# Attention of a two-layer encoder: copies alternate bank by bank between ScalarE and VectorE, one reciprocal per group, a new order of the score matmuls, and four engines in program order

## The chip, the cores and the metric

The kernel runs on one core of a Trainium2 chip. The metric is the device time of one execution in microseconds (us). Before the change the median of three runs is 2476.0 us (2475.49 to 2480.37).

## What is computed

One step of a two-layer encoder on 1024 prompt rows and 32 sample rows of width 1024: layer 0 has a matrix-memory mixer and an MLP, layer 1 a banded attention and an MLP. The change is in the attention. Each chunk of 64 queries sees its own 64 keys and the 512 before them; 16 query heads share 4 key/value heads (4 query heads to one), of width 64:

```python
def one_chunk(args):
    ci, qb = args
    kb = lax.dynamic_slice_in_dim(kp, ci * CHUNK, span, axis=1)
    vb = lax.dynamic_slice_in_dim(vp, ci * CHUNK, span, axis=1)
    s = jnp.einsum('bqkgd,bskd->bkgqs', qb, kb).astype(jnp.float32) * (HD_B ** -0.5) + bias
    valid = (ci * CHUNK - BAND + jnp.arange(span)) >= 0
    s = jnp.where(valid, s, -jnp.inf)
    p = jax.nn.softmax(s, axis=-1).astype(vb.dtype)
    return jnp.einsum('bkgqs,bskd->bqkgd', p, vb)
```

The 32 sample rows are treated as one more chunk against 512 cached keys and their own 32.

## The kernel before

The kernel is one program: layer 0, the projections q, k and v, the attention, its output projection, and layer 1's MLP. TensorE makes the matmuls, ScalarE (ACT) and VectorE (DVE) empty PSUM and do the softmax, GpSimd (POOL) normalises, and SP issues the loads.

The attention runs over `gp` (two pairs of key heads) and, within one, over 17 chunks `c` (16 is the sample chunk). The list `wide, slim` sets the order: wide chunks (8 to 15, with 576 keys) alternate with slim ones (0 to 7 with 64 to 512 keys, and 16), so gp 0 runs 8, 7, 12, 6, 13, 5, 14, 4, 15, 16, 9, 3, 10, 2, 11, 1, 0. A chunk has two groups, `e` = 0 and 1, one for each key head. A group has two units of 128 rows (two query heads by 64 queries; the sample chunk has one unit). So there are 34 chunks, 68 groups and 132 units.

For each unit, `softmax_unit` makes: the scores `s` (TensorE, two matmuls for each part, since q and k are kept as a high and a low part; a width over 512 takes two PSUM banks), a VectorE instruction that adds the bias and takes the row's minimum of the negated, scaled sum into `mx` (L1569, called the bias instruction below), the exponential with its row sum on ScalarE (L1572), a reciprocal of that sum on VectorE (L1573), and the multiplication by it on GpSimd (L1574). The scores have two PSUM buffers, so a unit's matmuls wait until the bias instruction of the unit two before has read its buffer.

For each group, `transposed` turns the probabilities `p` in blocks of 128 keys on TensorE into `pt`, two blocks of keys to a PSUM bank, with three such buffers; a copy then brings each bank to SBUF (`pT`). All copies of a group with e = 0 are VectorE's (L1598), all with e = 1 ScalarE's (L1596). A wide group has five key tiles, so three banks (0, 1 and 2); a slim group one to three.

For each chunk, `weighted_values` multiplies `pT` of both groups with V into `pv` (one PSUM buffer), key tile by key tile with the two groups in turn; every matmul shows as two instructions. ScalarE casts the result to a high part (L1613), and VectorE subtracts that for the low part (L1614).

`Flow` sets the order: a group is added as a generator, and each tick goes on with all groups, oldest first. So in step n stand the values of the chunk whose second group is n-4, then the transposes of group n-3, then the scores of group n. Only TensorE keeps this order (`manual_schedule`); for ScalarE, VectorE and GpSimd a scheduler sets the order when the program is built. Twice in gp 1, `wo_block` loads a block of the output weights (raw_ob) and splits it into two parts (w_ob) for the projection that follows.

Of the kernel before, what the change touches and what calls it, by code (L numbers as in the profile page):

```python
# [8 lines left out]
F32 = mybir.dt.float32  # L9
F32R = mybir.dt.float32r  # L10
# [65 lines left out]
def trunk_kernel(ctx: ExitStack, tc: tile.TileContext, a, o):  # L76
# [7 lines left out]
    def raw_tile(shape, name):  # L84
        return ring.tile(shape, F32, tag="raw", name=name, bufs=3)

    def split(dst_h, dst_l, src, eng=None):

        nc.scalar.copy(dst_h, src)
        (eng or nc.vector).tensor_sub(dst_l, src, dst_h.bitcast(F32))  # L90
# [706 lines left out]
    def tmp_t(shape, name, dt=F32):  # L797
        return T_.tile(shape, dt, tag="t", name=name, bufs=5)
# [299 lines left out]
    class Rooms:  # L1098


        def __init__(self):
            self.free = []
# [309 lines left out]
    def qo(c):  # L1412
        return QOT[c // 6][:, :, :, c % 6, :]
# [135 lines left out]

    nun = [0]  # L1550

    def softmax_unit(qst, g, k0, nk, bt, off, nm):

        s = psT.tile([P, 2, 512], F32, tag="s", name=f"s_{nm}", bufs=2)
        parts = [(0, 0, nk)] if nk <= 512 else [(0, 0, nk // 2), (1, nk // 2, nk // 2)]
        for b, j0, w in parts:
            for i in range(2):
                nc.tensor.matmul(s[:, b, :w], qst, kk[i][:, g, k0 + j0:k0 + j0 + w], start=(i == 0), stop=(i == 1))  # L1558
# [9 lines left out]
        mx = at.tile([P, 4], F32, tag="mx", name=f"mx_{nm}", bufs=8)  # L1568
        nc.vector.tensor_tensor_reduce(out=z.rearrange("p (b w) -> p b w", b=np_), in0=s[:, :np_, :w],  # L1569
                                       in1=bt.rearrange("p (b w) -> p b w", b=np_), op0=ALU.add, op1=ALU.min,  # L1570
                                       scale=-0.125, scalar=3e38, accum_out=mx[:, 0:1])
        nc.scalar.activation(z, z, AF.Exp, bias=mx[:, 0:1], scale=-1.0, accum_out=mx[:, 2:3])  # L1572
        nc.vector.reciprocal(mx[:, 3:4], mx[:, 2:3])  # L1573
        nc.gpsimd.tensor_scalar(z, z, mx[:, 3:4], 1.0, op0=ALU.mult, op1=ALU.mult)  # L1574
        return p

    def transposed(ps_, wid, e, nm):

        nt = (wid + P - 1) // P
        nq = len(ps_) * P  # L1580
        pt_sb = ring.tile([P, 5, 256], F32, tag="wc", name=f"pT_{nm}_{e}", bufs=6)
        for j0 in range(0, nt, 2):
            pt = psT.tile([P, 2, 256], F32, tag="pt", name=f"pt_{nm}_{e}_{j0}", bufs=3)
            js = range(j0, min(nt, j0 + 2))
            for j in js:
                kp = min(P, wid - j * P)
                for pr in range(len(ps_)):
                    nc.tensor.transpose(pt[:kp, j - j0, pr * P:(pr + 1) * P], ps_[pr][:, j * P:j * P + kp], ident)  # L1588
            if wid >= (js[-1] + 1) * P:
                jss = [(j0, len(js), P)]  # L1590
            else:
                jss = [(j, 1, min(P, wid - j * P)) for j in js]
            for j, m, kp in jss:
                dst, src = pt_sb[:kp, j:j + m, :nq], pt[:kp, j - j0:j - j0 + m, :nq]
                if e:
                    nc.scalar.copy(dst, src)  # L1596
                else:
                    nc.vector.tensor_copy(dst, src)  # L1598
        return pt_sb

    def weighted_values(gp, pts, nq, wid, vt0, dst, nm):
        nt = (wid + P - 1) // P
        pv = psT.tile([P, 256], F32, tag="pv", name=f"pv_{nm}", bufs=1)
        for j in range(nt):
            kp = min(P, wid - j * P)
            for e in range(2):
                g = 2 * gp + e
                nc.tensor.matmul(pv[64 * e:64 * e + 64, :nq], V[:kp, vt0 + j, g * 64:(g + 1) * 64], pts[e][:kp, j, :nq],  # L1608
                                 start=(j == 0), stop=(j == nt - 1))
# [3 lines left out]
        nc.scalar.copy(hi, src)  # L1613
        nc.vector.tensor_sub(lo, src, hi.bitcast(F32))  # L1614

    def att_group(gp, c, e):

        g = 2 * gp + e
        nm = f"{gp}_{c}"
        if c < 16:  # L1620
            nk = min(c + 1, 9) * 64
            k0 = max(0, c - 8) * 64
            off = k0 % P
            wid, vt0 = off + nk, (k0 - off) // P
            pr_ = [softmax_unit(qo(c)[:, e, gp, pr * P:(pr + 1) * P], g, k0, nk, bias[2 * g + pr][:, 576 - nk:], off,
                                f"{nm}_{e}{pr}") for pr in range(2)]
        else:
            wid, vt0 = 544, 8
            pr_ = [softmax_unit(qo(16)[:, e, gp, 0:P], g, TP, 544, sbias[g], 0, f"{nm}_{e}")]
        yield  # L1630
        yield
        yield
        pts[gp, c, e] = transposed(pr_, wid, e, nm)
        yield
        if e:
            if c < 16:
                dst = lambda hl: qo(c)[:, hl, gp, :]
            else:
                dst = lambda hl: qo(16)[:, hl, gp, :].rearrange("p (r i) -> p r i", i=64)[:, :, :TS]
            weighted_values(gp, [pts[gp, c, i] for i in range(2)], len(pr_) * P, wid, vt0, dst, nm)  # L1640
    pts = {}
    wo = a["w_out_b"][0]
    wo_pre = {}

    def wo_block(pr, half):
        cols = wo[:, 256 * pr:256 * pr + 256]
        return wtile(f"ob{pr}_{half}", lambda raw: [
            (raw[64 * e:64 * e + 64], cols[(2 * half + e) * 256:(2 * half + e + 1) * 256].rearrange(
                "(r d) c -> d r c", d=64)) for e in range(2)])

    wide, slim = (8, 12, 13, 14, 15, 9, 10, 11), ((7, 6, 5, 4, 16, 3, 2, 1, 0), (16, 7, 6, 5, 4, 3, 2, 1, 0))
    with tc.manual_schedule(engines={mybir.EngineType.PE}):
        for gp in range(2):
            for i in range(17):
                c = slim[gp][i // 2] if i % 2 else wide[i // 2] if i < 16 else slim[gp][8]
                for e in range(2):
                    flow.add(att_group(gp, c, e))
                    flow.tick()  # L1660
                if gp and i in (8, 11):
                    wo_pre[0, len(wo_pre)] = wo_block(0, len(wo_pre))
        flow.finish()
    psT_cm.__exit__(None, None, None)
    at_cm.__exit__(None, None, None)
    kv_cm.__exit__(None, None, None)
# [132 lines left out]
```

## Time and profile before

| | us |
|---|---|
| median of three runs | 2476.0 |
| the profiled execution | 2479.81 |
| its span | 2478.0 |
| attention, from the first scores to the first matmul of the output projection | 1422.1 to 1632.1 |
| TensorE busy, over the span | 2413.7 |

The profile gives starts in us from the start of the span. A busy TensorE is not one at its peak, since a matmul's shown length overlaps with the next one's; how fast it goes is read from the starts. The chain of waits follows the work that ended last back from the end, and so shows at each moment which engine is waited for. PE is TensorE's matmuls, PEld its weight loads.

### The profile page before, as it was taken

To read this page: it belongs to the slowest core of one execution; us is meant where nothing else is said; L and a number is where in the kernel's file an instruction comes from. 1 tells how busy PE (TensorE), PEld (TensorE's weight loads), DVE (VectorE), ACT (ScalarE), POOL (GpSimd) and SP (SyncE) were. 2 spreads that over 40 slices of the span, in tenths; PEclk is the share of its full clock that TensorE was granted. 3 is DMA by queue.
4 is the path that set the end of the run, shared out by engine and by line. 5 is a ranking of instruction groups with operands and counts; after the bars stand their busy time and mean duration, and the time that the engine had idled before them with its cause. 6 is when DMAs were issued, how large, how long until landed. Compare 5 with 4: busy or idle time off the path is not lost.

```text
span 2478.0 us, 42688 instructions
## 1 busy us (share of the span) xinstructions
PE 2413.7 (97%) x16844; PEld 2315.4 (93%) x16844; DVE 1759.7 (71%) x4038; ACT 1016.9 (41%) x2118; POOL 168.6 (7%) x315
## 2 busy tenths in 40 slices
PE   7999999999999999999999999999999999999997
PEld 4999999999999999999999867789999999899997
DVE  4899999788679679677597667746853442776758
ACT  4644456382211212212266556654754443221212
POOL 0211100000000000000001134410000000000003
PEclk9999999999999999999999989999999999999999
DMA  8433224313224224234122310050375646767632
GB/s 297 122 110 101 84 88 129 107 35 119 77 87 137 84 86 135 80 92 142 43 98 82 91 40 1 18 147 27 134 251 212 215 179 254 262 239 273 255 130 72
DMA packets 236220, 318.10 MB, mean 128 GB/s; under 512 B 11624, under 2 KB 185084, under 8 KB 234996
## 3 DMA queue, kind: packets, MB, share of 16 engines
q1 hardware_dynamic: 236020, 315.38, 38.8%
q8 instruction: 132, 2.16, 0.4%
q14 instruction: 68, 0.56, 0.1%
HBM read 242.79 MB, written 74.91 MB: 128 GB/s over the span
## 4 chain that ended last, share of the span: by engine, by line
PE 78%; DVE 8%; DMA 6%; ACT 2%; issue 1%; POOL 0%; SPq 0%; DVEq 0%; POOLq 0%; ACTq 0%
PE up L118 10%; PE up L120 10%; PE up L119 9%; PE dn L1283 9%; PE dn L119 5%; PE dn L118 5%; PE dn L120 5%; DMA fx<-hd 3%; PE pv L1608 2%; PE pt L1588 2%; PE s L1558 2%; PE o L118 1%; PE o L119 1%; PE o L120 1%; PE op_b L118 1%
## 5 line engine op out<-in xcount | busy, mean ns | idle before, releaser
L120 PE MATMUL up<-u,w_up 128*128 128x264 f32 x1024 | 292.9, 286 | 0.0
L118 PE MATMUL up<-u,w_up 128*128 128x264 f32 x1024 | 292.4, 286 | 0.0
L119 PE MATMUL up<-u,w_up 128*128 128x264 f32 x1024 | 291.1, 284 | 0.0
L1283 PE MATMUL dn<-fx,wf 128*128 128x264 f32 x2208 | 275.3, 286 | 7.9 <-DMA fx<-hd 7.4
L1283 PEld LDWEIGHTS dn<-fx,wf 128*128 128x128 f32 x2208 | 272.2, 189 | 9.7 <-issue 4.6
L119 PE MATMUL dn<-h,w_dn 128*128 128x384 f32 (+1 forms) x768 | 249.5, 325 | 0.0
L118 PE MATMUL up<-U,w_up 128*128 128x384 f32 (+1 forms) x768 | 249.2, 324 | 0.0
L119 PE MATMUL up<-U,w_up 128*128 128x384 f32 (+1 forms) x768 | 247.9, 323 | 0.0
L118 PE MATMUL dn<-h,w_dn 128*128 128x384 f32 (+1 forms) x768 | 247.8, 323 | 0.0
L120 PE MATMUL up<-U,w_up 128*128 128x384 f32 (+1 forms) x768 | 247.6, 322 | 0.0
L120 PE MATMUL dn<-h,w_dn 128*128 128x384 f32 (+1 forms) x768 | 247.3, 322 | 0.0
L119 PEld LDWEIGHTS up<-u,w_up 128*128 128x128 f32 x1024 | 193.9, 189 | 0.0
L118 PEld LDWEIGHTS up<-u,w_up 128*128 128x128 f32 x1024 | 193.8, 189 | 0.0
L120 PEld LDWEIGHTS up<-u,w_up 128*128 128x128 f32 x1024 | 193.3, 189 | 0.0
L986 DVE SCALAR_TENSOR_TENSOR ACC<-dn,ada,ACC 128x264 f32<-128x264 f32 (+4 forms) x328 | 131.7, 426 | 86.4 <-PE dn L1283 74.6
L238 DVE SCALAR_TENSOR_TENSOR aacc<-rada,cs,aacc 128x256 f32<-128x256 f32 x448 | 190.3, 477 | 0.0
L986 DVE SCALAR_TENSOR_TENSOR acc<-dn,ada,acc 128x384 f32<-128x384 f32 (+2 forms) x256 | 119.4, 486 | 47.4 <-PE dn L120 46.3
L1025 ACT ACTIVATE r<-up 128x384 f32<-128x384 f32 (+1 forms) x96 | 44.3, 463 | 246.9 <-PE up L120 238.4
L119 PEld LDWEIGHTS dn<-h,w_dn 128*128 128x128 f32 x768 | 144.4, 188 | 0.2 <-DVE h L1028 0.2
L120 PEld LDWEIGHTS dn<-h,w_dn 128*128 128x128 f32 x768 | 144.5, 188 | 0.0
L120 PEld LDWEIGHTS up<-U,w_up 128*128 128x128 f32 x768 | 144.3, 188 | 0.0
L118 PEld LDWEIGHTS up<-U,w_up 128*128 128x128 f32 x768 | 144.2, 188 | 0.1
(354 smaller groups left out, 5957.4 us busy)
## 6 DMA issues: line engine op xcount, KB each, us to landing
hd<-HL SPq DMA_DIRECT2D x28, 1848.0 KB
raw_up<-in_w_up_dram SPq DMA_DIRECT2D x68, 512.0 KB
rada<-in_w_ada_dram SPq DMA_DIRECT2D x64, 512.0 KB
fx<-hd SPq DMA_DIRECT2D x37, 528.0 KB
raw_dn<-in_w_down_dram SPq DMA_DIRECT2D x36, 512.0 KB
ada_room<-in_w_ada_dram SPq DMA_DIRECT2D x32, 512.0 KB
fx<-hd SPq DMA_DIRECT2D x50, 264.0 KB
fx<-hd SPq DMA_DIRECT2D x16, 792.0 KB
```

The source lines that it names most:

```text
L118: nc.tensor.matmul(ps, wh, mov(0, k), start=(k == 0), stop=False)
L119: nc.tensor.matmul(ps, wh, mov(1, k), start=False, stop=False)
L120: nc.tensor.matmul(ps, wl, mov(0, k), start=False, stop=(k == nk - 1))
L238: nc.vector.scalar_tensor_tensor(acc[:, cnd], raw[:, k], sc, acc[:, cnd], op0=ALU.mult, op1=ALU.add)
L986: nc.vector.scalar_tensor_tensor(xs, ps[:, off + o:off + o + mm_], gate[:, fc, cnd:cnd + 1], xs, op0=ALU.mult, op1=ALU.add)
L1025: nc.scalar.activation(r, ps[:, :n], AF.Relu)
L1283: nc.tensor.matmul(p, ws[w][:, wl, k], t[:, s0, xl], start=first and k + n_ == 0, stop=k == kg - 1 and n_ == 2, skip_group_check=not first)
L1558: nc.tensor.matmul(s[:, b, :w], qst, kk[i][:, g, k0 + j0:k0 + j0 + w], start=(i == 0), stop=(i == 1))
L1588: nc.tensor.transpose(pt[:kp, j - j0, pr * P:(pr + 1) * P], ps_[pr][:, j * P:j * P + kp], ident)
L1608: nc.tensor.matmul(pv[64 * e:64 * e + 64, :nq], V[:kp, vt0 + j, g * 64:(g + 1) * 64], pts[e][:kp, j, :nq], start=(j == 0), stop=(j == nt - 1))
```

## The change

It does five things in the attention, and none elsewhere:

- The copies of transposed banks alternate between ScalarE and VectorE bank by bank, by a counter, whichever group they belong to.
- There is one reciprocal for a group, on two columns, in `normalize`. It is issued in the next step, behind the first unit's scores of the next group.
- The group's second unit of scores stands on TensorE between the first and the second bank of the older group's transposes.
- The values of a chunk come first in a step, ahead of the step's scores; before, they were ahead of the transposes, but the scores of the step before stood between them and the last transposes.
- ScalarE, VectorE and GpSimd keep program order too.

With it go 11 buffers of probabilities in turn where there were 12, one tile of `mx` for a group (6 buffers) where there was one for a unit (8), and loads of the output weights that are issued two rounds ahead of their split. The core of the diff:

```diff
-        i = nun[0] % 12
-        p = tmp_t([P, 640], f"p_{nm}") if i < 5 else raw_tile([P, 640], f"p_{nm}") if i < 8 else \
+        i = nun[0] % 11
+        p = tmp_t([P, 640], f"p_{nm}") if i < 5 else raw_tile([P, 640], f"p_{nm}") if i < 7 else \
...
-        nc.scalar.activation(z, z, AF.Exp, bias=mx[:, 0:1], scale=-1.0, accum_out=mx[:, 2:3])
-        nc.vector.reciprocal(mx[:, 3:4], mx[:, 2:3])
-        nc.gpsimd.tensor_scalar(z, z, mx[:, 3:4], 1.0, op0=ALU.mult, op1=ALU.mult)
-        return p
+        nc.scalar.activation(z, z, AF.Exp, bias=mx[:, 0:1], scale=-1.0, accum_out=mx[:, 1:2])
+        return p, z
+
+    def normalize(units, mx):
+
+        n = len(units)
+        nc.vector.reciprocal(mx[:, 2, :n], mx[:, 1, :n])
+        for i, (_, z) in enumerate(units):
+            nc.gpsimd.tensor_scalar(z, z, mx[:, 2, i:i + 1], 1.0, op0=ALU.mult, op1=ALU.mult)
...
-                if e:
+                ncopy[0] += 1
+                if ncopy[0] % 2:
                     nc.scalar.copy(dst, src)
                 else:
                     nc.vector.tensor_copy(dst, src)
-        return pt_sb
+            yield pt_sb
+    ncopy = [0]
...
-    with tc.manual_schedule(engines={mybir.EngineType.PE}):
...
+    with tc.manual_schedule(engines={ET.PE, ET.Activation, ET.DVE, ET.Pool}):
+        for n in range(len(todo) + 4):
+            new, old, done = n if n < len(todo) else None, groups.get(n - 3), groups.pop(n - 4, None)
+            if done and done.e:
+                done.values()
+            if new is not None:
+                groups[n] = Group(*todo[n][:3])
+                groups[n].scores(0)
+            if groups.get(n - 1):
+                normalize(groups[n - 1].units, groups[n - 1].mx)
+            turn = old.turn() if old else iter(())
+            next(turn, None)
+            if new is not None:
+                groups[n].scores(1)
+            for _ in turn:
+                pass
+            if new is not None and todo[n][3] == "load":
...
+                for dst, src in wo_srcs(wo_raw, 0, len(wo_pre)):
+                    nc.sync.dma_start(dst, src)
+            elif new is not None and todo[n][3]:
...
+                split(w[:, 0], w[:, 1], wo_raw)
```

What this does to the orders, at chunk 13 of gp 0. In a name, the first number is the chunk; in s, p and mx the digits that follow are group and unit (p_5_10 is chunk 5, group 1, unit 0), in pT the group, and in pt the group and the first key tile of the bank (0, 2 or 4 for banks 0, 1 and 2); the number at the end only tells buffers apart. On TensorE, up to the first values of chunk 13, there stood:

```order
L1588 MATMUL pt_13_1_4_15377<-ident,p_13_10_15267 128x128
L1588 MATMUL pt_13_1_4_15377<-ident,p_13_11_15279 128x128
L1558 MATMUL s_14_00_15381<-k_14100,QO_13704 128x288
L1558 MATMUL s_14_00_15381<-k_14101,QO_13704 128x288
L1558 MATMUL s_14_00_15381<-k_14100,QO_13704 128x288
L1558 MATMUL s_14_00_15381<-k_14101,QO_13704 128x288
L1558 MATMUL s_14_01_15392<-k_14100,QO_13704 128x288
L1558 MATMUL s_14_01_15392<-k_14101,QO_13704 128x288
L1558 MATMUL s_14_01_15392<-k_14100,QO_13704 128x288
L1558 MATMUL s_14_01_15392<-k_14101,QO_13704 128x288
L1608 MATMUL pv_13_15403<-pT_13_0_15329,V 64x256
L1608 MATMUL pv_13_15403<-pT_13_1_15364,V 64x256
```

Now there stands:

```order
L1559 MATMUL s_14_01_15356<-k_14100,QO_13704 128x288
L1559 MATMUL s_14_01_15356<-k_14101,QO_13704 128x288
L1559 MATMUL s_14_01_15356<-k_14100,QO_13704 128x288
L1559 MATMUL s_14_01_15356<-k_14101,QO_13704 128x288
L1594 MATMUL pt_13_1_2_15364<-ident,p_13_10_15233 128x128
L1594 MATMUL pt_13_1_2_15364<-ident,p_13_11_15252 128x128
L1594 MATMUL pt_13_1_2_15364<-ident,p_13_10_15233 128x128
L1594 MATMUL pt_13_1_2_15364<-ident,p_13_11_15252 128x128
L1594 MATMUL pt_13_1_4_15370<-ident,p_13_10_15233 128x128
L1594 MATMUL pt_13_1_4_15370<-ident,p_13_11_15252 128x128
L1616 MATMUL pv_13_15374<-pT_13_0_15314,V 64x256
L1616 MATMUL pv_13_15374<-pT_13_1_15349,V 64x256
```

The eight score matmuls of 14's first group have moved from the place right before the values of 13 to places between the transposes, and the last two banks of transposes now stand right before the values.

On ScalarE, from the cast of chunk 6's values to that of chunk 13's, there stood:

```order
L1613 CAST QO_13490<-pv_6_15318 128x256
L1596 COPY pT_13_1_15364<-pt_13_1_0_15365 128x512
L1596 COPY pT_13_1_15364<-pt_13_1_2_15371 128x512
L1572 ACTIVATE p_5_10_15349,mx_5_10_15350<-p_5_10_15349,mx_5_10_15350 128x384
L1572 ACTIVATE p_5_11_15358,mx_5_11_15359<-p_5_11_15358,mx_5_11_15359 128x384
L1596 COPY pT_13_1_15364<-pt_13_1_4_15377 128x256
L1572 ACTIVATE p_14_00_15386,mx_14_00_15387<-p_14_00_15386,mx_14_00_15387 128x576
L1572 ACTIVATE p_14_01_15397,mx_14_01_15398<-p_14_01_15397,mx_14_01_15398 128x576
L1613 CAST QO_13704<-pv_13_15403 128x256
```

Now there stands:

```order
L1621 CAST QO_13490<-pv_6_15293 128x256
L1572 ACTIVATE p_5_10_15308,mx_5_1_15304<-p_5_10_15308,mx_5_1_15304 128x384
L1603 COPY pT_13_0_15314<-pt_13_0_0_15315 128x512
L1572 ACTIVATE p_5_11_15324,mx_5_1_15304<-p_5_11_15324,mx_5_1_15304 128x384
L1603 COPY pT_13_0_15314<-pt_13_0_4_15333 128x256
L1572 ACTIVATE p_14_00_15343,mx_14_0_15337<-p_14_00_15343,mx_14_0_15337 128x576
L1572 ACTIVATE p_14_01_15361,mx_14_0_15337<-p_14_01_15361,mx_14_0_15337 128x576
L1603 COPY pT_13_1_15349<-pt_13_1_2_15364 128x512
L1621 CAST QO_13704<-pv_13_15374 128x256
```

The copies of group 1's banks 0 and 2 have gone to VectorE, those of group 0's banks 0 and 2 have come, and the copy of group 1's bank 1 has moved from the third place to the one right before the next cast, behind all four exponentials.

On VectorE, from the subtraction for chunk 6's values to the bias instruction of 14's second unit, there stood:

```order
L1614 TENSOR_TENSOR QO_13490<-pv_6_15318,QO_13490 128x256
L1598 COPY pT_13_0_15329<-pt_13_0_2_15336 128x512
L1598 COPY pT_13_0_15329<-pt_13_0_4_15342 128x256
L1569 ISA p_5_10_15349,mx_5_10_15350<-s_5_10_15346,bias_14913 128x384
L1569 ISA mx_5_10_15350 128x1
L1569 ISA p_5_11_15358,mx_5_11_15359<-s_5_11_15355,bias_14916 128x384
L1569 ISA mx_5_11_15359 128x1
L1569 ISA p_14_00_15386,mx_14_00_15387<-s_14_00_15381,bias_14913 128x576
L1569 ISA mx_14_00_15387 128x1
L1573 RECIPROCAL mx_5_10_15350<-mx_5_10_15350 128x1
L1569 ISA p_14_01_15397,mx_14_01_15398<-s_14_01_15392,bias_14913 128x576
```

Now there stands:

```order
L1622 TENSOR_TENSOR QO_13490<-pv_6_15293,QO_13490 128x256
L1569 ISA p_5_10_15308,mx_5_1_15304<-s_5_10_15305,bias_14913 128x384
L1569 ISA mx_5_1_15304 128x1
L1578 RECIPROCAL mx_5_0_15263<-mx_5_0_15263 128x2
L1569 ISA p_5_11_15324,mx_5_1_15304<-s_5_11_15321,bias_14916 128x384
L1569 ISA mx_5_1_15304 128x1
L1605 COPY pT_13_0_15314<-pt_13_0_2_15327 128x512
L1569 ISA p_14_00_15343,mx_14_0_15337<-s_14_00_15338,bias_14913 128x576
L1569 ISA mx_14_0_15337 128x1
L1578 RECIPROCAL mx_5_1_15304<-mx_5_1_15304 128x2
L1605 COPY pT_13_1_15349<-pt_13_1_0_15350 128x512
L1569 ISA p_14_01_15361,mx_14_0_15337<-s_14_01_15356,bias_14913 128x576
```

The rows with `mx` alone as their output bring the row minimum out. The bias instruction of chunk 5 has moved ahead of the copies, right behind the subtraction, and a reciprocal for both units of a group now stands ahead of a bank's copy.

More of the change, by code (lines that the diff above doesn't have):

```diff
@@ L1614, in weighted_values, with __init__ @@
         nc.vector.tensor_sub(lo, src, hi.bitcast(F32))
[L1616 to L1635, printed above, removed]
+    class Group:
+        def __init__(self, gp, c, e):
+            self.gp, self.c, self.e, self.g = gp, c, e, 2 * gp + e
+            self.nm = f"{gp}_{c}"
+            self.mx = at.tile([P, 3, 2], F32, tag="mx", name=f"mx_{self.nm}_{e}", bufs=6)
+            self.units = []
+            self.n = 2 if c < 16 else 1
@@ L1636, in att_group @@
             if c < 16:
[L1637 to L1640 removed]
+                self.nk, self.k0 = min(c + 1, 9) * 64, max(0, c - 8) * 64
+                self.off = self.k0 % P
+                self.wid, self.vt0 = self.off + self.nk, (self.k0 - self.off) // P
+            else:
+                self.nk, self.k0, self.off, self.wid, self.vt0 = 544, TP, 0, 544, 8
@@ new lines, in scores, with turn @@
+        def scores(self, pr):
+            if pr >= self.n:
+                return
+            bt = bias[2 * self.g + pr][:, 576 - self.nk:] if self.c < 16 else sbias[self.g]
+            self.units.append(softmax_unit(qo(self.c)[:, self.e, self.gp, pr * P:(pr + 1) * P], self.g, self.k0, self.nk,
+                                           bt, self.off, self.mx[:, :, pr], f"{self.nm}_{self.e}{pr}"))
+        def turn(self):
+            for pts[self.gp, self.c, self.e] in transposed([p for p, _ in self.units], self.wid, self.e, self.nm):
+                yield
@@ L1641, in trunk_kernel, with values @@
+        def values(self):
+            if self.c < 16:
+                dst = lambda hl: qo(self.c)[:, hl, self.gp, :]
+            else:
+                dst = lambda hl: qo(16)[:, hl, self.gp, :].rearrange("p (r i) -> p r i", i=64)[:, :, :TS]
+            weighted_values(self.gp, [pts[self.gp, self.c, i] for i in range(2)], self.n * P, self.wid, self.vt0, dst,
+                            self.nm)
     pts = {}
@@ L1653, in trunk_kernel @@
     wide, slim = (8, 12, 13, 14, 15, 9, 10, 11), ((7, 6, 5, 4, 16, 3, 2, 1, 0), (16, 7, 6, 5, 4, 3, 2, 1, 0))
-    with tc.manual_schedule(engines={mybir.EngineType.PE}):
[L1655 to L1663, printed above, removed]
+    todo = []
```

21 lines of the change are left out of this document (15 added, 6 removed).

## The prediction, made before the changed kernel was run

> **What bounds the kernel now.** I read the page's busy table first, then the busy times by stretch to find the attention stage, the groups of that stretch by shape, the chain of waits in order of time, and the timeline where an order matters.
>
> ```profile
> PE 2413.7 (97%) x16844; PEld 2315.4 (93%) x16844; DVE 1759.7 (71%) x4038; ACT 1016.9 (41%) x2118; POOL 168.6 (7%) x315
> ```
>
> Over the span TensorE is the bound. The stretches (us; busy PE, PEld, DVE, ACT, POOL; granted clock; DMA) say what the attention stage does:
>
> ```profile
> 1430.50:1457.00 26.50, 23.97 (x146) 17.84 (x146) 16.61 (x54) 15.21 (x39) 9.25 (x17) 0.83 0.19 42
> ...
> 1633.00:1660.00 27.00, 27.00 (x169) 27.00 (x168) 9.06 (x14) 19.34 (x30) 0.00 (x0) 1.00 1.02 268
> 1430.50:1633.00 202.50, 193.10 (x1409) 143.18 (x1410) 142.72 (x505) 132.41 (x376) 83.54 (x161) 0.98 0.07 16
> ```
>
> The stage is about 202 us, with VectorE busy 142.7 and ScalarE 132.4; right behind it (1633 to 1660) TensorE is full. So what the attention gains or loses shifts the rest of the span one for one. The chain of waits names how the stage goes chunk by chunk (start, us, what). Each chunk ends with its weighted values (pv):
>
> ```profile
> 1423.54 6.78 DMA bias<-bias_d
> ...
> 1441.27 3.27 PE pv L1608 x20
> ...
> 1462.03 2.03 PE pv L1608 x16
> 1464.05 1.24 PE pt L1588 x10
> 1465.29 0.70 PE s L1558 x4
> 1465.99 1.24 PE pt L1588 x10
> 1467.23 1.25 PE s L1558 x8
> 1468.48 2.31 PE pv L1608 x20
> 1470.79 0.82 PE pt L1588 x6
> ...
> 1471.61 0.57 DVE pT L1598
> ...
> 1474.59 1.65 PE pv L1608 x12
> ...
> 1514.43 1.06 PE s L1558 x8
> ...
> 1630.98 1.10 PE pv L1608 x4
> 1632.08 0.34 PE op_b L118
> ```
>
> From the end of pv of chunk 6 (1462.03 + 2.03 = 1464.06) to the end of pv of chunk 13 (1470.79) are 6.73 us, and every row in it is TensorE's: a wide chunk is already bound by TensorE. From there to the end of chunk 5's pv (1474.59 + 1.65 = 1476.24) are 5.45 us, with VectorE copies on the chain: a slim chunk still waits. From the first pv's end (1444.54) to the last one's (1632.08) are 187.5 us for 33 chunks, 15 wide and 18 slim.
>
> **The change, part by part.** The prices, from the groups by shape in 1430.5 to 1633 (busy us, mean ns | idle before):
>
> ```profile
> L1572 ACT ACTIVATE p<-p,mx 128x576 f32<-128x576 f32 x61 | 47.0, 773 | 6.8 <-DVE mx L1569 6.4
> L1574 POOL TENSOR_SCALAR p<-p,mx 128x576 f32<-128x576 f32 x61 | 45.4, 749 | 49.2 <-DVE mx L1573 47.3 <-PE pv L1608 1.4
> L1569 DVE CUSTOM_DVE_ANT_0 p<-s,bias 128x576 f32<-128x576 f32 x61 | 44.4, 748 | 10.5 <-PE s L1558 8.0 <-DMA bias<-bias_d 2.4
> L1598 DVE COPY pT<-pt 128x512 f32<-128x512 f32 x44 | 29.7, 684 | 5.5 <-PE pt L1588 5.5
> L1596 ACT COPY pT<-pt 128x512 f32<-128x512 f32 x44 | 25.0, 584 | 43.1 <-PE pt L1588 42.9
> L1573 DVE RECIPROCAL mx<-mx 128x1 f32<-128x1 f32 x129 | 20.3, 160 | 28.4 <-ACT p L1572 27.0
> L1614 DVE TENSOR_TENSOR QO<-pv,QO 128x256 fp32r<-128x256 f32 x32 | 13.3, 417 | 9.0 <-ACT QO L1613 8.9
> L1613 ACT CAST QO<-pv 128x256 fp32r<-128x256 f32 x32 | 11.7, 366 | 7.6 <-PE pv L1608 7.3
> L1598 DVE COPY pT<-pt 128x256 f32<-128x256 f32 x20 | 8.3, 416 | 2.8 <-PE pt L1588 2.8
> L1596 ACT COPY pT<-pt 128x256 f32<-128x256 f32 x20 | 7.2, 370 | 7.9 <-PE pt L1588 7.9
> L1572 ACT ACTIVATE p<-p,mx 128x384 f32<-128x384 f32 x8 | 4.9, 614 | 0.0
> ...
> L1569 DVE CUSTOM_DVE_ANT_0 p<-s,bias 128x384 f32<-128x384 f32 x8 | 4.3, 552 | 0.3
> ...
> L90 DVE TENSOR_TENSOR w_ob<-raw_ob,w_ob 128x1024 fp32r<-128x1024 f32 x2 | 2.4, 1221 | 0.0
> ```
>
> Reciprocals: 132 of one column become 68 of two. VectorE saves 64 x 0.160 = 10.2 us of work, and much of the 27 us in which it stood before a reciprocal for ScalarE. Neither is on the path of a wide chunk: worth at most what the slim chunks wait. Copies: 82 on each engine before and after, so no load moves; what moves is whose turn comes when. Buffers (11 probabilities in turn for 12, six mx tiles of a group for eight of a unit): nothing, since the buffer asked for belongs to a group whose transposes came two steps before. The zero fills and normalisations on GpSimd (83.5 us busy of 202.5) have two steps until the transposes: nothing; if that cover went, one 0.75 us normalisation per chunk. The weight block w_ob: its loads stay ahead of all else in SP's queue, and its split (1.22 us on VectorE) now stands at a fixed place before a chunk's pv, hidden behind that pv but for 0.4 us, twice: 0.8 us. The start waits for the bias load of 6.78 us either way: nothing. Behind the stage one or two more raw_ob issues stand ahead of the accumulator's loads on SP:
>
> ```profile
> 1632.70 0.67 SPq L96 DMA_DIRECT2D raw_ob<-in_w_out_b_dram  x1
> ```
>
> Eight PSUM banks take TensorE's first output blocks meanwhile (TensorE is full from 1633 to 1660, while the loads land): nothing, and two issues, 1.3 us, if that cover went.
>
> What costs is the order. Before, the next group's scores stood on TensorE between a chunk's last transposes and its pv, so VectorE and ScalarE worked on them during pv. After, pv follows the transposes directly, the result's cast and subtraction stand at the head of both queues until pv has ended, and ScalarE's copy of the chunk's middle bank stands behind two exponentials. The waiting times between engines, from the timeline (start, length, engine, line):
>
> ```profile
> 1465.29 0.41 DVE L1614 TENSOR_TENSOR QO<-pv,QO 128x256 fp32r<-128x256 f32 x1
> 1465.62 1.01 DVE L1598 COPY pT<-pt 128x512 f32<-128x512 f32 x2
> ...
> 1470.87 0.37 ACT L1613 CAST QO<-pv 128x256 fp32r<-128x256 f32 x1 [0.24 <-PE pv L1608]
> 1471.27 0.43 DVE L1614 TENSOR_TENSOR QO<-pv,QO 128x256 fp32r<-128x256 f32 x1 [0.45 <-ACT QO L1613]
> ```
>
> ```profile
> 1502.96 1.34 PE L1558 MATMUL s<-k,QO 128*128 128x288 f32 x8
> ...
> 1503.91 0.76 DVE L1569 CUSTOM_DVE_ANT_0 p<-s,bias 128x576 f32<-128x576 f32 x1 [0.66 <-PE s L1558]
> ...
> 1504.72 0.78 ACT L1572 ACTIVATE p<-p,mx 128x576 f32<-128x576 f32 x1
> ```
>
> The cast starts 0.1 us behind pv's end, the subtraction 0.4 later, and VectorE's next instruction 0.33 after that: 0.88 in all. An instruction frees its engine about 0.1 before its end. Scores of 576 columns can be read 0.95 after their first matmul starts, and the exponential follows the bias-and-minimum instruction's start by its length and 0.05. TensorE takes 0.116 a pv matmul (2.31 / 20), 0.124 a transpose, 0.133 a wide score.
>
> *A wide chunk, 13, after the end of pv of chunk 6 (= 0).* Scores of 5, head group 1: bias 0.88, exponential 1.48 to 2.09. Then ScalarE copies bank 0 of the first group, 2.09 to 2.68, does the second exponential of 5 (2.57 to 3.18) and bank 2 (to 3.55). TensorE issues the first scores of 14 at 1.9; bias 2.85, exponential 3.65 to 4.42. The second group's first transposes need the PSUM buffer that bank 0's copy frees at 2.68, so they go 2.74 to 3.24 and the second scores of 14 start at 3.24. VectorE has by then the reciprocal, the copy of the second group's bank 0 (3.60 to 4.29), and only then the bias for 14's second unit, 4.21; its exponential runs 5.01 to 5.78. Behind it stands ScalarE's copy of the second group's bank 1, 5.78 to 6.37. TensorE started pv at 4.52, did two of five key tiles by 5.45, and waits to 6.43; three tiles of 0.46 end at 7.82. That is 7.82 - 6.73 = +1.09.
>
> *A slim chunk, 5, after pv of 13.* Bias of 14's third unit 0.92; exponential 1.72 to 2.49; copy of 5's bank 0 to 2.97; exponential to 3.74; exponential of 4 to 4.30 (320 columns, estimated 0.56 from the 384 and 576 rows); copy of the second group's bank 0, 4.30 to 4.89. The second matmul of pv reads it: 4.95 + 10 x 0.116 = 6.1. That is +0.65 against 5.45.
>
> The same walk made with the old order for chunk 13 gives 6.6 where the trace has 6.73, so I trust one window to about 0.2. The sum: 15 x 1.09 + 18 x 0.65 = 16.4 + 11.7 = 28.1, and 0.8 for the splits, from which I leave off as much for the first chunk, whose transposes no longer delay the second pair of scores. Bounds: a window may be off by twice the 0.2 either way, 33 x 0.4 = 13, so +15 to +41 for the stage.
>
> Perfetto Trace Analysis in the Trainium skill (Identifying the Most-Contended Engine) speaks against this: for VectorE and ScalarE occupancy is a fair measure of how close they are to their limit. By that rule 70% and 65% leave room and the time would fall to the first rival's. I put the walk above it, because what costs is where an instruction stands in a queue, not the queue's load.
>
> **The rivals.**
> First, *faster: the copies are in time and TensorE never waits.* It decides at chunk 13's middle bank: if the second exponential of 14 starts by 3.9 rather than 5.0 us after the last pv, its copy ends before TensorE needs it. For it speaks that both engines have slack, against it the queue order. Then each chunk costs its own matmuls: chunk 5 two times 0.74 for transposes, 1.06 and some 0.64 for scores, 1.39 for pv = 4.57, that is 0.88 less, and chunk 13 6.5, 0.2 less: 18 x 0.88 + 15 x 0.2 = 19, so 2457.
> Second, *a wash*: slim chunks gain about what wide ones lose, within 5 us of 2476. For it: VectorE loses its waits for single exponentials. Against: chunk 5 has the same late copy.
> Third, *worse: the clock falls.* Here TensorE would stop about 1 us in every chunk. Stops there were before, too:
>
> ```profile
> 1528.00:1538.00 10.00, 8.61 (x64) 6.45 (x61) 7.98 (x30) 6.31 (x19) 4.51 (x8) 1.00 0.00 1
> ```
>
> In this stretch of small chunks TensorE stood 1.4 of 10 us and the granted clock stayed at 1.00; it was 0.83 only behind the long wait for the bias load. TensorE: Matmul & The Clock Gate in the Trainium skill (A second HAM failure mode) says that short idle times between groups of matmuls, often enough, make the clock swing; this trace does not show it. At 0.83 the matmuls on the walked path, 2.4 us of a wide chunk and 1.7 of a slim one, cost 0.5 and 0.35 more: 15 x 0.5 + 18 x 0.35 = 14, so about 2518. That the change doesn't do what it says can be left out: the orders above are those of the built programs.
>
> **How the numbers follow.** The profiled execution took 2479.8 us around a span of 2478.0, 0.15% above the median of 2476.0; the +28 holds for both: 2508 for an execution like it, 2504 for the median. Chances: the late copy (forecast) 0.77, never waiting 0.13, a wash 0.04, the clock 0.06. The forecast alone spans 2491 to 2517; to leave out no more than 2 in 10 the range reaches down to the wash and up over the clock's case: 2476 to 2521. A measurement of this kernel can tell about 0.2%, 5 us, from no change: faster 0.13, same 0.04, slower 0.83.
>
> **What would show it.** Right: pv's ends some 7.8 us (chunk 13) and 6.1 us (chunk 5) behind the ones before; before pv, TensorE idle for ScalarE's copies, about 1 us a chunk; ScalarE idle for pv in every chunk, 2 us or more until its first exponential; the stage some 28 us longer at a clock of 1.00. Wrong: windows at 6.5 and 4.6 with TensorE alone on the chain (first rival), or TensorE's clock well below 1 in mid-stage (third), or a difference behind the stage, which I hold to move as one.

## The result and the profile after

The changed kernel is slower: 2519.36 us in the median of 6 runs (2515.04 to 2526.07), against 2479.27 for the kernel before on the same chips (6 runs, 2475.49 to 2483.02). The ratio is 1.0167, with a 95% interval of 1.0157 to 1.0177, about 41 us. The profiled execution took 2517.58 us around a span of 2515.8.

The head of the page of the changed kernel, with the same columns as before:

```profile
span 2515.8 us, 42702 instructions
...
PE 2435.4 (97%) x16844; PEld 2325.8 (92%) x16844; DVE 1755.3 (70%) x3974; ACT 1022.1 (41%) x2118; POOL 164.4 (7%) x315
```

VectorE's and ScalarE's work is the same within 0.6%, and GpSimd's is a little less, so the 37.8 us by which the span has grown are no added work. The busy times by stretch of the changed kernel (us; busy PE, PEld, DVE, ACT, POOL; granted clock; DMA) show where they are:

```profile
1430.50:1457.00 26.50, 24.90 (x162) 18.29 (x163) 16.07 (x47) 16.45 (x41) 9.90 (x17) 0.94 0.21 45
...
1457.00:1600.00 143.00, 126.86 (x885) 90.44 (x884) 83.23 (x275) 84.63 (x233) 52.06 (x100) 1.00 0.02 5
1600.00:1630.00 30.00, 25.57 (x158) 17.96 (x156) 15.62 (x52) 15.90 (x43) 9.32 (x19) 0.89 0.07 18
1630.00:1660.00 30.00, 24.16 (x142) 16.47 (x141) 14.06 (x46) 14.96 (x40) 8.81 (x18) 0.88 0.08 19
...
1672.00:1700.00 28.00, 28.00 (x176) 28.00 (x175) 10.75 (x16) 19.06 (x30) 0.00 (x0) 1.00 0.89 241
```

The same stretch of 143 us in the kernel before:

```profile
1457.00:1600.00 143.00, 138.97 (x1048) 103.68 (x1045) 103.99 (x366) 96.92 (x273) 62.31 (x119) 1.00 0.03 9
```

At the same clock of 1.00, TensorE gets through 885 matmul records in these 143 us where it got through 1048, and VectorE is busy 83 us instead of 104. Everything is less busy, so they wait for each other. From 1600 on the clock is also lower, 0.89 and 0.88. Behind the stage TensorE is full again, as it was before.

Measured from cast to cast of pv (a window is the time from the cast of one chunk's values to that of the next chunk's): the 33 windows of the stage took 187.5 us before (first cast at 1444.62, last at 1632.12) and 231.2 after (1440.59 to 1671.77), 43.7 more. Of this the start gives back 4.0, since the first pv ends earlier (clock 0.94 in the first stretch where it was 0.83), and the rest of the span behind the last cast is 1.9 us shorter (844.0 for 845.9; the waits of the last matmuls for their loads, fx, are 5.6 us in place of 7.4). 43.7 - 4.0 - 1.9 = 37.8.

The chunk that the prediction walked through, 13 of gp 0, in the timeline of the changed kernel (start, length, engine, line; in brackets the idle time before and what ended it):

```profile
1462.92 0.37 ACT L1621 CAST QO<-pv 128x256 fp32r<-128x256 f32 x1 [1.35 <-PE pv L1616]
...
1464.26 0.62 ACT L1572 ACTIVATE p<-p,mx 128x384 f32<-128x384 f32 x1 [0.97 <-DVE mx L1569]
...
1467.33 1.51 PE L1616 MATMUL pv<-pT,V 128*64 128x256 f32 x10
1467.69 0.78 ACT L1572 ACTIVATE p<-p,mx 128x576 f32<-128x576 f32 x1 [0.51 <-DVE mx L1569]
1468.47 0.56 ACT L1603 COPY pT<-pt 128x512 f32<-128x512 f32 x1
1469.09 1.51 PE L1616 MATMUL pv<-pT,V 128*64 128x256 f32 x10 [0.25 <-ACT pT L1603]
1470.63 0.37 ACT L1621 CAST QO<-pv 128x256 fp32r<-128x256 f32 x1 [1.60 <-PE pv L1616]
1471.04 0.42 DVE L1622 TENSOR_TENSOR QO<-pv,QO 128x256 fp32r<-128x256 f32 x1 [3.04 <-ACT QO L1621]
```

This is the walked order. With pv's end 0.1 ahead of its cast, as in the walk, chunk 6's pv ends at 1462.82. From there the walk had the second 576-wide exponential of chunk 14 at 5.01 (measured 4.87), the copy of the middle bank behind it at 5.78 (5.65), the rest of pv at 6.43 (6.27) and its end at 7.82 (7.71). ScalarE idles 1.60 us ahead of the cast, and VectorE, whose subtraction is next in its queue, 3.04.

What ScalarE waited for in the changed kernel from 1430 to 1600 (us in all, times, longest):

```profile
ACT p L1572 <- DVE mx L1569: 38.4, 49, 2.4
ACT QO L1621 <- PE pv L1616: 30.2, 22, 1.8
```

In the kernel before:

```profile
ACT pT L1596 <- PE pt L1588: 44.7, 27, 2.2
ACT p L1572 <- DVE mx L1569: 8.7, 7, 3.4
ACT QO L1613 <- PE pv L1608: 5.4, 11, 1.5
```

VectorE waited for the cast with its subtraction, in the changed kernel:

```profile
DVE QO L1622 <- ACT QO L1621: 55.4, 23, 3.2
```

In the kernel before:

```profile
DVE QO L1614 <- ACT QO L1613: 6.3, 10, 1.7
```

Before, ScalarE waited for transposes, that is, it was ahead of TensorE. Now it waits for pv with its cast, and after that for the bias instruction that VectorE could not begin either, since VectorE stands at its subtraction.

### The profile page after: what moved, and what is told of

Read it like the earlier page. It is cut to its first block, busy times and chain, and to the rows that moved or that the text cites. A ratio compares the mean times of both kernels' runs of the same rounds, so it can differ in the third digit from the quotient of the medians.

```text
span 2515.8 us, 42702 instructions
## 1 busy us (share of the span) xinstructions
PE 2435.4 (97%) x16844; PEld 2325.8 (92%) x16844; DVE 1755.3 (70%) x3974; ACT 1022.1 (41%) x2118; POOL 164.4 (7%) x315
## 3 DMA queue, kind: packets, MB, share of 16 engines
q1 hardware_dynamic: 236020, 315.38, 37.8%
## 4 chain that ended last, share of the span: by engine, by line
PE 78%; DVE 9%; ACT 3%; DMA 3%; issue 2%; POOL 0%; SPq 0%; DVEq 0%; ACTq 0%; POOLq 0%
PE dn L1283 11%; PE up L118 10%; PE up L120 10%; PE up L119 10%; PE dn L119 5%; PE dn L118 5%; PE dn L120 5%; PE pv L1616 2%; DVE p L1569 1%; DMA fx<-hd 1%; PE o L118 1%; PE o L119 1%; PE o L120 1%; ACT p L1572 1%; PE op_b L118 1%
```

## The experiments

The theory behind the forecast: pv stands right behind the transposes, and under program order the cast and the subtraction block their queues during pv, while the copies that pv needs stand behind exponentials. Against it stand three others: that TensorE's new order costs by itself (B), that program order as such costs (C), and that the clock falls (D). And two sizes are to be settled: the splits of the weight block, and the place of pv. All ratios are against the kernel before on the same chip. Gains in us are differences from the 2519.36 of the changed kernel, which ran at another time; the interval of each ratio is 2 to 4 us to either side.

**Only TensorE keeps program order**

```diff
-    with tc.manual_schedule(engines={ET.PE, ET.Activation, ET.DVE, ET.Pool}):
+    with tc.manual_schedule(engines={ET.PE}):
```

> The changed kernel, but only TensorE keeps program order; ScalarE, VectorE and GpSimd get the scheduler's order back. The order puts the copy of chunk 13's middle bank ahead of the second exponential of 14, and the copies ahead of the split of the output weights. Theory A (the late copy behind exponentials, and the splits at a bad place, cost the time; TensorE's new order does not by itself): about 25 us of the 41 come back, 2490 to 2498. Rival B (TensorE's new order, with pv right behind the transposes, is the cost, whatever the other queues do): at most 10 us come back, above 2508. Rival C (program order as such is the cost): all of it comes back, 2475 to 2484.

Measured: 2477.84 us (2475.32 to 2483.38), ratio 0.9995 [0.9986, 1.0005]. All of the loss is gone. TensorE's new order by itself is refuted as the cause, and so, under the scheduler's order, are the alternation, the late reciprocal and the buffers. The time is the one that rival C named (2475 to 2484), and the next run decides on C. The 2490 to 2498 of the first theory are missed: I had thought that part of the loss lies in pv's place, whatever the other engines do. In its timeline ScalarE, around the same chunk, has:

```profile
1467.10 0.78 ACT L1572 ACTIVATE p<-p,mx 128x576 f32<-128x576 f32 x1 [0.35 <-DVE mx L1569]
...
1467.88 0.56 ACT L1603 COPY pT<-pt 128x512 f32<-128x512 f32 x1
1468.44 0.78 ACT L1572 ACTIVATE p<-p,mx 128x576 f32<-128x576 f32 x1
```

The scheduler put the copy between the two wide exponentials, not behind both. The chain of this run has pv as one piece, though it starts before that copy does:

```profile
1467.78 2.38 PE pv L1616 x20
```

**Program order on all four engines, TensorE's old order**

```diff
-            if new is not None:
-                groups[n] = Group(*todo[n][:3])
-                groups[n].scores(0)
+            for _ in old.turn() if old else ():
+                pass
             if groups.get(n - 1):
                 normalize(groups[n - 1].units, groups[n - 1].mx)
-            turn = old.turn() if old else iter(())
-            next(turn, None)
             if new is not None:
+                groups[n] = Group(*todo[n][:3])
+                groups[n].scores(0)
                 groups[n].scores(1)
-            for _ in turn:
-                pass
```

> The changed kernel with TensorE's old order: in a step the values, then all transposes, then both units' scores. Alternating copies, one late reciprocal per group and program order on four engines stay, and so does the place of the splits in the step. Theory A: a wide chunk is bound by TensorE again, about 6.5; a slim one waits for the copy behind its neighbour's exponentials, 5.9 against 5.45; with 6 for the splits 2484 to 2492. Rival C (program order as such is the cost): above 2508.

Measured: 2483.86 us (2480.59 to 2486.21), ratio 1.0020 [1.0011, 1.0030]. Of the 41 us, 5 are left, with program order still on all engines: rival C is refuted. The chain is TensorE's again, with scores between the last transposes and pv:

```profile
1463.39 1.09 PE pt L1594 x10
1464.48 1.05 PE s L1559 x8
1465.53 2.31 PE pv L1616 x20
```

What remains sits in two windows of gp 1, those of chunks 15 and 3, in which a weight block is split: 10.35 and 7.68 us, where the windows at the same places in gp 0 take 6.23 and 5.07. The next run takes that away:

```diff
-            todo += [(gp, c, e, gp and e and {7: "load", 9: "split", 10: "load", 12: "split"}.get(i)) for e in range(2)]
+            todo += [(gp, c, e, gp and not e and {7: "load", 9: "split", 10: "load", 12: "split"}.get(i)) for e in range(2)]
```

> The run with TensorE's old order and program order on four engines, with the loads and splits of the output weights one step earlier, so that a split no longer stands between the copies of a chunk's two groups. Theory A' (program order and TensorE's new order cost only together; the splits' place cost the 6.7 us by which the windows of chunks 15 and 3 in gp 1 exceed those in gp 0): 6 to 7 us off, 2476 to 2479, no different from before. Rival (the splits' time only moves to VectorE's bias instructions behind them): 2481 to 2484.

Measured: 2476.09 us (2471.47 to 2477.78), ratio 0.9981 [0.9973, 0.9990]; the two windows are 6.51 and 5.52. Program order with the old order on TensorE and the splits one group earlier is, if anything, faster than the kernel before.

**The changed kernel with the splits one group earlier**, the same line alone:

> The changed kernel; the loads and the two splits of the output weights each stand one step earlier, so that a split comes behind all copies of a chunk and right ahead of its pv, not between the copies of its two groups. Theory A (the split's place costs 6 us, and the stop of over 3 us that it makes brings the clock down in the 60 us behind it, 5 us more): 2507 to 2510, granted clock 0.97 or more from the first split to the end of the stage. Rival D (the clock falls because TensorE stops about 1 us in every chunk): 2512 to 2514, the clock behind as low as before, 0.8 to 0.9.

Measured: 2513.20 us (2511.67 to 2515.22), ratio 1.0138 [1.0122, 1.0153]: about 6 us gained, not the 10 to 12 expected, and inside rival D's 2512 to 2514. The two windows fall as they should (from 11.71 to 8.25 and from 8.06 to 5.81), and in the stretches right behind the two splits the clock no longer falls (0.99 or more from 1608 to 1651). But it falls elsewhere, to 0.63 in 1651 to 1660, and already in gp 0 of this run:

```profile
1530.00:1535.00 5.00, 4.54 (x23) 3.58 (x24) 2.03 (x10) 2.81 (x12) 2.18 (x4) 0.66 0.00 0
```

In the changed kernel the same stretch was granted 1.00:

```profile
1530.00:1535.00 5.00, 4.06 (x26) 2.66 (x26) 2.65 (x16) 3.40 (x12) 2.18 (x4) 1.00 0.00 0
```

So rival D holds in part, and in other places from one profiled execution to the next. The stop of TensorE ahead of this stretch is 1.38 us, no longer than in the changed kernel (both are shown at the end).

**Copies ahead of the exponential.** The bias instruction and the exponential of a group's second unit are issued behind the older group's last copies (its scores stay where they are):

```diff
+        yield
         nun[0] += 1
...
             if new is not None:
                 groups[n] = Group(*todo[n][:3])
                 groups[n].scores(0)
+                groups[n].soft(0)
...
             for _ in turn:
                 pass
+            if new is not None:
+                groups[n].soft(1)
```

> The changed kernel; the bias instruction and the exponential of a group's second unit are issued behind the older group's last copies instead of ahead of them. TensorE's order is as in the changed kernel, and all four engines keep program order. Theory A: a wide chunk no longer waits for its middle bank, 7.8 becomes about 6.9, slim chunks stay: 15 x 0.9 = 13, so 2503 to 2508; the splits still cost. Rival B: the wait only moves to the bias instruction and the next scores, within 5 us of 2519.

Measured: 2508.05 us (2505.64 to 2512.89), ratio 1.0113 [1.0096, 1.0130], 11 us gained, at the upper edge of the 2503 to 2508 expected. Chunk 13's window falls from 7.71 to 6.92, and its pv goes in one piece in the chain of this run:

```profile
1470.16 2.46 PE pv L1617 x20
```

So the late copy made 0.79 of the 1.04 by which chunk 13's window had grown, as walked. Of all seven wide windows of gp 0 it is half: 0.51 of 1.04 each are left. The slim windows gain nothing (on average of gp 0 they are 1.10 longer than before the change, where the changed kernel's are 0.99 longer), in part perhaps since the clock fell here to a half:

```profile
1530.00:1535.00 5.00, 5.00 (x22) 3.49 (x21) 1.42 (x8) 1.89 (x6) 1.60 (x4) 0.50 0.01 3
```

**Pv one unit later**, behind the first scores of its step:

```diff
-            if done and done.e:
-                done.values()
             if new is not None:
                 groups[n] = Group(*todo[n][:3])
                 groups[n].scores(0)
+            if done and done.e:
+                done.values()
```

> The changed kernel with one edit: the values of a chunk stand one unit of scores later in the step, behind the first unit of the next group. From the runs so far (copies first took 11 us off, the moved splits 6, and all three edits together 29) theory A' expects 10 to 14 us off by this edit alone: 2505 to 2509. Rival (the three edits only work together): less than 5 us off, above 2514.

Measured: 2496.95 us (2494.51 to 2497.94), ratio 1.0076 [1.0058, 1.0094]: 22 us gained where 10 to 14 were expected. Pv's place right behind the transposes is worth over half of the loss under program order. This edit is the one that helps the slim windows: those of gp 0 are 0.27 longer than before the change in place of 0.99, and the wide ones 0.56 in place of 1.04. The waits of this run for what stops pv and the cast (1430 to 1600):

```profile
PE pv L1616 <- ACT pT L1603: 2.6, 6, 0.8
...
ACT QO L1621 <- PE pv L1616: 16.2, 19, 1.3
```

In the changed kernel the first was

```profile
PE pv L1616 <- ACT pT L1603: 9.5, 21, 1.1
```

and the second, shown above, 30.2 in 22 times. With one unit of scores between transposes and pv, ScalarE has the time for its copy, and its queue is held for less long.

**The three together** (copies first, pv later, splits earlier):

> The changed kernel with three edits: copies ahead of the second unit's exponential, splits one step earlier, and the values of a chunk one unit of scores later, so that VectorE and ScalarE have a unit's bias and exponential to do during pv. TensorE's interleaving of scores and transposes stays. Theory A' (the order pv right behind the transposes leaves both engines with nothing to do for 2 us a chunk): wide windows from 6.9 to 6.6, slim ones from 6.6 to 5.9, 2484 to 2492. Rival (interleaving the scores with the transposes is itself the cost): above 2498.

Measured: 2490.06 us (2487.64 to 2493.96), ratio 1.0043 [1.0028, 1.0059], as expected. The single edits gained 11.3, 22.4 and 6.2 us, 40 in sum, and 29 together. Copies first and pv later may in part cure the same wait; that is not shown. What the windows do show is that the splits still cost in this run. With pv later, a split that stands one group earlier comes to fall into the windows of chunks 5 and 9 in gp 1 (its halves on VectorE start at 1590.83 and 1612.28): these are 8.13 and 9.54, where gp 0 has 5.91 and 6.73, some 5 us. So of the 10 us that are left, about half may be the splits'; the rest, at most, is this order of TensorE's work under program order.

**Parts of the change alone, in the kernel before** (a scheduler still sets the order of ScalarE, VectorE and GpSimd). Alternating copies:

```diff
-                if e:
+                ncopy[0] += 1
+                if ncopy[0] % 2:
                     nc.scalar.copy(dst, src)
```

> The kernel before with one part of the change alone: the copies alternate between ScalarE and VectorE bank by bank; all else, the scheduler's order included, as before. Theory A' (who copies matters little as long as a copy is not behind a waiting instruction): within 5 us of before. Rival (the alternation itself puts copies behind exponentials): 10 us or more above.

Measured: 2474.86 us (2467.57 to 2476.46), ratio 0.9974 [0.9964, 0.9984]. A small gain. In the profiled execution, 2467.57 and so the fastest of them, the first pv is done 6 us earlier (cast at 1438.58), at a clock of 0.94 in the first stretch, so not all of it need be the copies'.

One reciprocal for a group, late, with the tile of mx for a group:

```diff
-        nc.vector.reciprocal(mx[:, 3:4], mx[:, 2:3])
-        nc.gpsimd.tensor_scalar(z, z, mx[:, 3:4], 1.0, op0=ALU.mult, op1=ALU.mult)
-        return p
+        return p, z
...
+        normalize(pr_, mx)
+        pr_ = [p for p, _ in pr_]
```

> The kernel before with one part of the change alone: one reciprocal for a group, on two columns, issued behind both units' exponentials, with the scheduler's order for it; copies and TensorE's order as before. Theory A': 10 us of VectorE work saved, none of it on the path, within 5 us of before. Rival (VectorE's waits before single reciprocals were what held the slim chunks): 8 us or more below before, near 2470.

Measured: 2480.11 us (2477.78 to 2483.81), ratio 1.0006 [0.9996, 1.0015]: no difference. The 10 us of VectorE's work that it saves are not on the path.

**A version that follows from this**: the run with the old order of TensorE and the earlier splits, and in it the exponentials one step later, behind the next step's copies, with the reciprocal behind the next group's bias instructions.

```diff
-        nc.scalar.activation(z, z, AF.Exp, bias=mx[:, 0:1], scale=-1.0, accum_out=mx[:, 1:2])
         return p, z
...
+        for i, (_, z) in enumerate(units):
+            nc.scalar.activation(z, z, AF.Exp, bias=mx[:, 0, i:i + 1], scale=-1.0, accum_out=mx[:, 1, i:i + 1])
+        yield
         nc.vector.reciprocal(mx[:, 2, :n], mx[:, 1, :n])
```

> Built on the old order of TensorE with program order on four engines and the splits one step earlier: the exponentials of a group move one step later, behind the next step's copies, and its reciprocal behind the next group's bias instructions. No copy stands behind an exponential that is not yet ready. Theory A' (the copy behind a waiting exponential is what slim chunks pay): wide windows stay at 6.5, slim ones fall from 5.9 to 4.9 or less: 18 x 0.6 = 11 below the run that differs only by this, 2464 to 2470. Rival (slim chunks are held by the chain from scores over bias, exponential and reciprocal to the transposes, which gets longer): no gain, 2476 or above, with TensorE waiting for GpSimd.

Measured: 2469.07 us (2466.77 to 2470.28), ratio 0.9956 [0.9943, 0.9968]; faster than both kernels, by 11 us than the one before on the same chip (2479.90) and by 7 than the run that it builds on, where 11 were expected. The slim windows of gp 0 are 0.87 shorter each than in that run, the wide ones 0.24 longer. In its chain from chunk 6's pv on nearly all is TensorE's:

```profile
1460.71 1.24 PE pt L1596 x10
1461.96 0.71 PE s L1559 x4
1462.67 1.09 PE pt L1596 x10
1463.76 1.05 PE s L1559 x8
1464.81 2.31 PE pv L1618 x20
1467.12 0.80 PE pt L1596 x6
1467.92 0.54 PE s L1559 x4
1468.60 0.76 DVE p L1569
```

Chunk 13's window is 6.40, chunk 5's 4.99. What TensorE still waited for from 1430 to 1600:

```profile
PE s L1559 <- DVE mx L1569: 2.6, 7, 1.5
PE pt L1596 <- POOL p L1582: 1.4, 3, 0.7
```

ScalarE waits for pv with its cast for as long as in the changed kernel:

```profile
ACT QO L1623 <- PE pv L1618: 34.4, 26, 2.4
```

Here it costs nothing: the copies that pv reads are done, and the exponentials that follow are not due for a step.

## Why the prediction was right, and where a size was off

**The direction and the mechanism** were right. Slower was given 0.83, and 2519.4 lies in the range, but near its upper end, and that is partly luck. The forecast was +28 us, and +40 came, 1 us inside the +15 to +41 of the walk. As a time, 2519.4 is above the 2491 to 2517 of the walk; the range reached 2521 only to take in the clock's case. The terms that were short are the splits, the slim chunks and the clock, below.

The mechanism needs both halves, pv right behind the transposes and program order: each of them alone costs nothing (0.9995 and, with the splits moved, 0.9981). Putting the copies first, or pv one unit later, takes back 11 and 22 us. The signs that were named came too. In 22 of the 23 chunks that end between 1430 and 1600, ScalarE idled ahead of its cast. TensorE's weight loads for pv waited 18.7 us in 22 times for ScalarE's copies, 0.85 each, where about 1 us a chunk was forecast (before: 0.4 us, once). The matmul rows show only 9.5 of this. The clock was at 1.00 until 1600 and fell behind that.

**The wide chunk**, forecast at +1.09: chunk 13's window is 7.71 in gp 0 and 7.83 in gp 1, for 7.82 forecast. The seven wide windows of gp 0 are 7.26 us longer than before, 1.04 each.

**The slim chunk**, forecast at +0.65: chunk 5's window is 6.36 and 6.32, for 6.1. In gp 0 that is 0.69 more than before (5.67); in gp 1, where it took 6.17 before, 0.15. The nine of gp 0 are 8.95 us longer, 0.99 each: this term was too small by a third of a us a chunk, about 6 in 18, because one chunk stood for all, and chunks 2, 4 and 16, among others, lost 1.82, 1.27 and 1.26. They were not walked through.

**The split, the step that failed.** "Its split (1.22 us on VectorE) now stands at a fixed place before a chunk's pv, hidden behind that pv but for 0.4 us, twice: 0.8 us." The timeline of the changed kernel has it like this:

```profile
1610.59 1.05 ACT L89 CAST w_ob<-raw_ob 128x1024 fp32r<-128x1024 f32 x1
1611.67 1.23 DVE L90 TENSOR_TENSOR w_ob<-raw_ob,w_ob 128x1024 fp32r<-128x1024 f32 x1 [1.75 <-ACT w_ob L89]
1612.82 0.75 DVE L1569 CUSTOM_DVE_ANT_0 p<-s,bias 128x576 f32<-128x576 f32 x1
...
1613.57 0.67 DVE L1605 COPY pT<-pt 128x512 f32<-128x512 f32 x1
...
1614.30 1.29 PE L1616 MATMUL pv<-pT,V 128*64 128x256 f32 x8 [1.88 <-DVE pT L1605]
```

It stands between the two groups of a chunk, so the chunk's second set of copies, which pv reads, is behind it. And it isn't 1.22 us: VectorE's half waits for ScalarE's cast of the block, with 1.75 us of idle time ahead of it, and then takes 1.23; with it wait the bias instruction and the copy. The Trainium skill says the same of the queues (PSUM — Partial Sum Buffer, Engine vs sequencer instructions: those of ScalarE, VectorE and GpSimd are strict FIFO); these rows agree. The two windows are 11.71 and 8.06, while those at the same places in gp 0 take 7.48 and 5.72: 4.2 + 2.3 = 6.5 us where 0.8 was forecast. Over 1 us of the 4.2 comes by the lower clock: the last ten matmuls of this pv took 2.82 us, those of chunk 13's pv 1.51.

**The clock**, the third rival, given 0.06, comes in as a second term. Around the two splits, by stretch of the changed kernel:

```profile
1608.00:1616.00 8.00, 5.55 (x40) 3.91 (x38) 5.47 (x15) 4.81 (x12) 2.34 (x7) 0.94 0.19 52
1616.00:1625.00 9.00, 8.04 (x38) 5.55 (x38) 3.58 (x13) 3.92 (x11) 2.31 (x5) 0.67 0.07 14
...
1634.00:1642.00 8.00, 4.68 (x29) 3.17 (x28) 4.47 (x13) 4.51 (x11) 2.81 (x4) 1.00 0.00 1
1642.00:1651.00 9.00, 8.39 (x53) 6.83 (x52) 4.27 (x14) 4.51 (x12) 2.04 (x8) 0.81 0.22 51
1651.00:1660.00 9.00, 7.32 (x37) 4.25 (x34) 3.80 (x15) 3.87 (x12) 3.02 (x5) 0.78 0.06 10
```

TensorE stood 2.45 and 3.3 us in the stretches of the splits, and in those behind them the clock was 0.67, 0.81 and 0.78. The windows of chunks 4, 10, 2 and 11 in gp 1 are 0.8, 1.6, 0.9 and 1.2 us longer than in gp 0: 4.5 us. With moved splits the time fell by 6, not by 6.5 + 4.5: in that run other windows grew, near the places where its clock fell (chunk 11 by 1.0 us in gp 0 and by 0.8 in gp 1, chunk 8 of gp 1 by 1.6). So the clock is not the splits' alone, and how much of the time is its is not settled.

**The sum.** 43.7 us of longer windows are 6.5 for the splits, 4.5 for the windows behind them, and 32.7 for the rest, where 28.1 was forecast. The start, held to be worth nothing, gave back 4.0 in the profiled execution; the clock in the first stretch was 0.83 before, 0.94 after and 0.87 with copies first, which may be the reason; no run isolates it. "Moves as one" behind the stage holds to 2 us.

**Edits costed at nothing.** The late reciprocal was (1.0006, the interval holds 1). The alternation of copies, whose load the prediction left unmoved, is a small gain by itself.

**The first rival**, no waits at all and 2457, was not reached here. The late exponentials with TensorE's old order come within 12 us of it, 2469.

## What to carry to other kernels

An instruction that waits holds all that stands behind it in its engine's queue, so when an order is fixed by hand, put the copies that the next matmuls read ahead of work whose result is due later (exponentials, splits), and leave other matmuls between the producers of a copy and its reader. A step in two halves on two engines, put into two queues at the same point, holds the second queue until both halves are done, here for 1.75 + 1.23 us. What that costs depends on what stands behind it: 4.2 and 2.3 us ahead of copies that pv reads, and 0.8 and 0.1 one group earlier, right ahead of pv. Judge each half of such a change with the other half undone: here two halves that cost 0 and 5 us by themselves cost 41 together.

## What was not expected of the hardware

The granted clock is not a fixed answer to a stop. The changed kernel and the one with moved splits have the same order in gp 0, and their windows agree there within 0.01 us up to chunk 10. Ahead of chunk 2's pv TensorE makes the same stop in both, here in the changed kernel:

```profile
1530.07 0.44 PE L1559 MATMUL s<-k,QO 128*128 128x128 f32 x2 [1.38 <-DVE mx L1569]
```

And with the splits moved:

```profile
1528.92 0.44 PE L1559 MATMUL s<-k,QO 128*128 128x128 f32 x2 [1.38 <-DVE mx L1569]
```

In both a second stop of 0.53 us follows, and with the copies first there are the same two stops. Yet in 1530 to 1535 the clock was 1.00 in the changed kernel, 0.66 with the splits moved and 0.50 with the copies first. The rule on short idle times between groups of matmuls (TensorE: Matmul & The Clock Gate in the Trainium skill, A second HAM failure mode), which the trace of before did not show, agrees with these runs in that the clock swings, with means over 5 to 9 us between 0.50 and 0.94. What decides whether a stop brings the clock down stays open; no run here isolates it.
